# Weight sums of the third and fourth pair in the first feed-forward block: begun by ScalarE and DMA at the fetch instead of VectorE later

## The chip, the cores and the metric

The kernel runs on one core of a Trainium2 chip. A core has five engines that run their own queues in order: TensorE (PE, with its weight loads PEld), VectorE (DVE), ScalarE (ACT), GpSimd (POOL) and SyncE (SP). SP and POOL are used here to issue DMA transfers; a transfer that POOL issues can add what it reads to what already lies at its destination (an accumulating transfer). The metric is the device time of one execution in microseconds (us). One execution was also profiled, and its trace is what is read below.

## The reference

A bidirectional encoder trunk of two layers over 512 tokens and 16 learned meta tokens, width 1024, all in float32. Each layer is a feed-forward block, a mixer (gated linear attention beside softmax attention) and a second feed-forward block. What matters here is the feed-forward block, of which four run in one execution:

```python
def swiglu(x, w_gate, w_up, w_down):
    return (jax.nn.silu(x @ w_gate) * (x @ w_up)) @ w_down
...
    for l in range(DEPTH):
        h = h + 0.5 * swiglu(rmsnorm(h, norm_gains[l, 0]),
                             ffn_w_gate[l, 0], ffn_w_up[l, 0], ffn_w_down[l, 0])
        h = h + mixer(rmsnorm(h, norm_gains[l, 1]), w_in[l], gla_w2[l], gla_b2[l], gla_gn[l],
                      q_norm[l], k_norm[l], w_pa[l], w_pb[l], b_merge[l], w_out[l], cos, sin)
        h = h + 0.5 * swiglu(rmsnorm(h, norm_gains[l, 2]),
                             ffn_w_gate[l, 1], ffn_w_up[l, 1], ffn_w_down[l, 1])
    return rmsnorm(h, final_norm)[:, N_META:]
```

The inner width is 2816, which is 22 blocks of 128 columns.

## The kernel before

**Seven products instead of eight.** The 22 blocks of the inner width are taken as 11 pairs, numbered 0 to 10 (`NPAIR`); so the first four pairs are 0, 1, 2 and 3. For each pair the gate and up weights are cut into four tiles of 128 x 1024 that the host has laid out in DRAM: "11", "12", "21" and "22". Instead of eight products of these with the four parts of the input, seven products of sums are made, named "1" to "7". Product 1 takes tile 11, product 2 tile 12, product 4 tile 22. The other four take weight sums that the kernel makes on the chip:

- first sum, for product 5: s1 = 21 + 22
- third sum, for product 7: s3 = 21 - 11
- second sum, for product 6: s2 = 22 + s3
- fourth sum, for product 3: s4 = s2 - 12

The down projections of the first two groups of four pairs are done alike, as four-tile sets numbered 11 to 14.

**From float32 to the matrix unit.** Each of the seven operands becomes two tiles before TensorE reads it: ScalarE rounds it to a high part (`whi`, line 287) and VectorE subtracts that from the operand for a low part (`wlo`, line 288). One product is 24 matmuls (4 parts of the input, 2 halves, and hi x hi, hi x lo, lo x hi), with the two hi matmuls ahead of the first that reads `wlo`.

**Order.** `ffn_steps` writes the order of the products by hand. In the first block (layer 0, first feed-forward: `(0, 0)`) it begins, as (pair, product): (0,1) (0,2) (1,1) (1,2) (0,4) (1,4) (0,6) (0,5) (0,7) (0,3) (1,6) (1,5) (2,1) (1,7) (2,2) (1,3) (2,6) (2,5) (3,1) (2,7) (3,2) (2,4) (2,3) (3,6) (3,5) (3,7) and so on. The class `Weights` runs ahead of it: `use` makes the hi and lo parts 3 operands ahead of the product in hand (`make`) and fetches 9 ahead (`fetch`). A compile-time scheduler then sets the order on each engine's queue: by the order in the program, but passing over what it takes to be not ready yet by its own model of times. What it sets is fixed; on the chip each queue runs in that order and waits where something is late.

**Buffers.** Three raw tiles (`wraw`), three "long" tiles (`wsa`: s3 and s4 of the pairs) and three "short" tiles (`wsb`: s1 and s2). A new tile takes the place of one that is done with. In the first block the tile of s3 of pair 2 follows that of s4 of pair 0, which is free when product (0,3) has its `wlo`; that of s3 of pair 3 follows s3 of pair 1, free at the `wlo` of (1,7).

**How the sums are made.** There are two ways:

- Chained, for pairs 0 and 1 of every block: ScalarE writes s3 = -11 (`negative`, line 203); POOL issues a transfer that adds tile 21 from DRAM (line 208); tile 22 is loaded by SP as s2, and a second POOL transfer adds s3 to it. ScalarE also begins s4 as -12, and a third POOL transfer adds s2.
- By VectorE, for pairs 2 to 10: SP loads tile 21 as s3 (line 218) and tile 22 as s2 (line 219); when product 2's parts have been made VectorE subtracts tile 11 from s3 (line 253), which keeps tile 11 in its raw buffer until then; ahead of product 6's parts VectorE adds s3 to s2 (line 297), and behind them makes s4 (line 256).

In both, s1 is tile 21 loaded by SP with a POOL transfer that adds tile 22 (`first_sum`). In the pairs 0 and 1 of the first block the sums are begun when product 1's and 2's parts are made; in all others, `begin_sums` runs at the fetch of tile 11.

Of the kernel before, what the change touches and what calls it, by code (L numbers as in the profile page):

```python
# [148 lines left out]
NPAIR = FF // P // 2  # L149
# [21 lines left out]
class Weights:  # L171
# [34 lines left out]
    def add(self, t, src):  # L206

        self.nc.gpsimd.dma_start(t, src, accum_op=ALU.add)  # L208

    def begin_sums(self, f, i, w=None):  # L210

        got = self.summed
        s3 = None
        if i < 2:
            s3 = self.negative(f, i, "s3", w)
            self.add(s3, self.dram(f, i, "21"))
        elif i < NPAIR:
            s3 = self.block(f, i, "21", self.long, "wsa")
        s2 = self.block(f, i, "22", self.short, "wsb")
        if i < 2:  # L220
            self.add(s2, s3)
        got[f, i, "7"], got[f, i, "6"] = s3, s2
        if (f, i) not in OPENING:
            self.first_sum(f, i)
# [6 lines left out]
    def sums(self, f, i, product, w):  # L231


        got, V = self.summed, self.nc.vector
        if (f, i) in OPENING and product in "12":
            (self.begin_sums if product == "1" else self.first_sum)(f, i, *[w] * (product == "1"))
        if i < 2:
            if product == "2":
                s4 = self.negative(f, i, "s4", w)
                self.add(s4, got[f, i, "6"])  # L240
                got[f, i, "3"] = s4
        elif product == "1":
            if i < NPAIR:
                self.kept1 = w
            else:
                got[f, i, "7"] = self.negative(f, i, "s3", w)
                self.add(got[f, i, "7"], self.dram(f, i, "21"))
            if not i < NPAIR:
                self.add(got[f, i, "6"], got[f, i, "7"])
        elif product == "2":  # L250
            self.kept = w
            if i < NPAIR:
                V.tensor_tensor(got[f, i, "7"], got[f, i, "7"], self.kept1, ALU.subtract)
        elif product == "6":
            s4 = self.long.tile([P, SLAB], F32, tag="wsa", name=f"s4_{f[0]}{f[1]}_{i}")
            V.tensor_tensor(s4, w, self.kept, ALU.subtract)
            got[f, i, "3"] = s4
# [15 lines left out]
    def make(self, upto):  # L273
        nc = self.nc
        while self.made < min(upto, len(self.loads)):
            self.fetch(self.made + 1)
            s = self.made
            load = self.loads[s]
            w = self.raws.pop(s, None)
            if w is None:  # L280
                w = self.summed.pop(load)
            hi = self.hi_pool.tile([P, SLAB], F32R, tag="whi", name=f"whi{s}")
            lo = self.lo_pool.tile([P, SLAB], F32R, tag="wlo", name=f"wlo{s}")
            for a in np.split(np.arange(SLAB), 2 if s == 0 else 1):
                cs = slice(a[0], a[-1] + 1)
                with self.tc.issue_after(self.behind) if self.behind else nullcontext():
                    nc.scalar.copy(hi[:, cs], w[:, cs])  # L287
                nc.vector.tensor_tensor(lo[:, cs], w[:, cs], hi[:, cs].bitcast(F32), ALU.subtract)  # L288
            self.got[s] = (hi, lo)
            self.got.pop(s - 12, None)  # L290
            self.made += 1
            if not isinstance(load, int) and load[2] in "126":
                self.sums(*load, w)
            after = self.loads[s + 1] if s + 1 < len(self.loads) else 0
            if not isinstance(after, int) and after[2] == "6" and 2 <= after[1] < NPAIR:
                s2, s3 = [self.summed[after[:2] + (c,)] for c in "67"]
                nc.vector.tensor_tensor(s2, s2, s3, ALU.add)

# [30 lines left out]
def build(tc, ctx, xt, wts, win, par, w2, const, umask, out):  # L329
# [243 lines left out]
    def ffn(l, f, norm, done, following):  # L573

        x, rs, up, n = norm.x, None, None, live[0]
        w = n // 2
        pools = open_pools("left", psum=("s2",), c=4, s2=2)
        made, hid, sums, raw, sets = {}, {}, {}, {}, {}
        risen = iter(range(KC))

# [637 lines left out]
    def finish_chunk(c):  # L1218
        fin.square(c)
        gain(c, slice(0, SEQ))  # L1220

    def ending(sums, operand, rs):

        table("abs_reciprocal_sqrt_and_small")
# [146 lines left out]
```

## Time and profile before

| | |
|---|---|
| time, median of 3 runs | 2212.42 us (2210.72 to 2214.04) |
| the profiled execution's own time | 2211.05 us |
| its span, first to last instruction | 2209.2 us |
| DVE busy | 1785.4 us (81%) |
| ACT busy | 1214.1 us (55%) |
| POOL busy | 101.8 us (5%) |
| the first 40 us: DMA busy share of 16 engines | 0.92 and 1.05 in its two halves |

The profile gives for each instruction its start and duration in us, its engine, its line in the kernel, the operation, and the tiles as out<-in with their buffer numbers left out; so `wlo<-w,whi` is the low part of some operand `w`, and several kinds of tile share the name `w`. Behind a row, in brackets, stands how long the engine had been idle just before, and what ended that idle time. `SPq` and `ACTq` rows are DMA issues by an engine's sequencer. In the table by windows the columns are the stretch, its length, then the busy time and number of instructions of PE, PEld, DVE, ACT and POOL, the granted TensorE clock (1.00 is full speed), the mean busy share of the 16 DMA engines and GB/s.

### The profile page before, as it was taken

Reading aid. Unit: us, or ns where it says so; the run is one execution under the profiler, and the core shown is the slowest. Engines: PE = TensorE matmul, PEld = TensorE weight load, DVE = VectorE, ACT = ScalarE, POOL = GpSimd, SP = SyncE. Lnnn points to the kernel's source line nnn. Section 1 sums busy time; section 2 is a strip of 40 time slices with the busy share of each in tenths; the row PEclk is TensorE's granted clock in tenths of the full one; section 3 lists DMA queues with packets and bytes.
Section 4 is the critical chain, followed back from the end, with each engine's and each line's share of the span. In section 5 each row is a group of like instructions: output and inputs, shape, how many; then the busy total and the mean of one; then the engine's idle time right before and its main releaser. Section 6 shows DMA issues by size and latency. Waiting matters only on the chain.

```text
span 2209.2 us, 40079 instructions
## 1 busy us (share of the span) xinstructions
PE 2162.4 (98%) x16506; PEld 2070.2 (94%) x16506; DVE 1785.4 (81%) x2703; ACT 1214.1 (55%) x1779; POOL 101.8 (5%) x120
## 2 busy tenths in 40 slices
PE   7999999999999999999999999999999999999998
PEld 6999999989999999999999999999788888999997
DVE  7897978486886689889789979775879767997987
ACT  7544545344785555454575445453457836554543
POOL 1000000000000001000010000000000001000100
PEclk9999999999999999999999999999999999999999
DMA  9775753212113468666567757432121145776752
GB/s 268 189 204 160 191 152 106 82 49 68 49 39 122 114 167 205 190 182 187 162 163 186 207 164 191 143 110 77 49 84 51 42 133 152 198 202 181 189 165 67
DMA packets 87463, 311.41 MB, mean 141 GB/s; under 512 B 9712, under 2 KB 12144, under 8 KB 87280
## 3 DMA queue, kind: packets, MB, share of 16 engines
q1 hardware_dynamic: 68624, 245.53, 32.9%
q0 software_dynamic: 16704, 60.82, 15.8%
q8 instruction: 130, 2.13, 0.4%
q10 hardware_dynamic: 1952, 2.50, 0.4%
q14 instruction: 53, 0.43, 0.1%
HBM read 289.94 MB, written 2.10 MB: 132 GB/s over the span
## 4 chain that ended last, share of the span: by engine, by line
PE 81%; DVE 11%; ACT 4%; issue 2%; DMA 2%; SPq 0%; DVEq 0%; ACTq 0%
PE ss L598 37%; PE mm L465 13%; PE ss L712 11%; PE ss L465 10%; PE sm L465 2%; DVE wlo L288 2%; DMA w<-win 2%; PE sm L1074 1%; PE ss L1049 1%; DVE g L678 1%; ACT whi L287 1%; PE sm L1090 1%; DVE h L720 1%; PE ss L471 1%; PE sm L1091 1%
## 5 line engine op out<-in xcount | busy, mean ns | idle before, releaser
L598 PE MATMUL ss<-xc,whi 128*128 128x264 f32 (+1 forms) x4928 | 907.2, 285 | 15.5 <-ACT whi L287 7.4
L598 PEld LDWEIGHTS ss<-xc,whi 128*128 128x128 f32 x4928 | 767.2, 189 | 20.4 <-ACT c L602 8.4
L598 PE MATMUL ss<-xc,wlo 128*128 128x264 f32 (+1 forms) x2464 | 702.5, 285 | 8.8 <-DVE wlo L288 8.8
L598 PEld LDWEIGHTS ss<-xc,wlo 128*128 128x128 f32 x2464 | 466.5, 189 | 11.1 <-DVE wlo L288 10.9
L288 DVE TENSOR_TENSOR wlo<-w,whi 128x1024 fp32r<-128x1024 f32 (+1 forms) x337 | 408.1, 1217 | 63.4 <-ACT whi L287 63.2
L287 ACT CAST whi<-w 128x1024 fp32r<-128x1024 f32 (+1 forms) x337 | 350.0, 1050 | 163.3 <-PE ss L598 80.5
L465 PE MATMUL mm<-x,whi 128*128 128x264 f32 (+1 forms) x1712 | 384.6, 315 | 0.0
L465 PEld LDWEIGHTS mm<-x,whi 128*128 128x128 f32 x1712 | 278.3, 188 | 16.5 <-issue 1.0
L465 PE MATMUL mm<-x,wlo 128*128 128x264 f32 (+1 forms) x856 | 266.0, 315 | 0.0
L712 PE MATMUL ss<-g,whi 128*128 128x264 f32 (+1 forms) x1280 | 237.4, 284 | 0.0
L287 ACT CAST whi<-raw 128x1024 fp32r<-128x1024 f32 x126 | 132.3, 1050 | 163.4 <-PE mm L465 102.3
L602 ACT COPY c<-ss 128x528 f32<-128x528 f32 (+1 forms) x132 | 78.5, 594 | 258.6 <-PE ss L598 258.6
L288 DVE TENSOR_TENSOR wlo<-raw,whi 128x1024 fp32r<-128x1024 f32 x126 | 153.9, 1222 | 59.0 <-ACT whi L287 58.1
L712 PEld LDWEIGHTS ss<-g,whi 128*128 128x128 f32 x1280 | 198.4, 188 | 0.1
L712 PE MATMUL ss<-g,wlo 128*128 128x264 f32 (+1 forms) x640 | 181.3, 283 | 0.0
L465 PEld LDWEIGHTS mm<-x,wlo 128*128 128x128 f32 x856 | 159.6, 188 | 8.5 <-issue 0.7
L465 PE MATMUL ss<-g,whi 128*128 128x264 f32 (+2 forms) x900 | 166.3, 299 | 0.0
L465 PEld LDWEIGHTS ss<-g,whi 128*128 128x128 f32 x900 | 131.7, 188 | 5.3
L208 POOL DMA_DIRECT2D w<-win x60 | 52.7, 878 | 1574.7 <-DVE wlo L288 582.5
L712 PEld LDWEIGHTS ss<-g,wlo 128*128 128x128 f32 x640 | 120.5, 188 | 0.0
L444 ACT ACTIVATE c<-c 128x528 f32<-128x528 f32 (+1 forms) x88 | 56.6, 643 | 98.5 <-DVE c L642 98.4
L465 PE MATMUL ss<-g,wlo 128*128 128x264 f32 (+2 forms) x450 | 106.2, 300 | 0.0
(267 smaller groups left out, 3370.2 us busy)
## 6 DMA issues: line engine op xcount, KB each, us to landing
w<-win SPq DMA_DIRECT2D x335, 512.0 KB, 4.5
raw<-wts SPq DMA_DIRECT2D x126, 512.0 KB, 3.3
w<-win POOLq DMA_DIRECT2D x60, 512.0 KB, 7.4
s<-win POOLq DMA_DIRECT2D x24, 512.0 KB, 7.2
w<-s POOLq DMA_DIRECT2D x24, 512.0 KB, 5.6
s<-w POOLq DMA_DIRECT2D x8, 512.0 KB, 9.6
h<-xt SPq DMA_DIRECT2D x3, 528.0 KB, 6.8
out<-h ACTq DMA_DIRECT2D x4, 256.0 KB, 2.4
```

Of the source, the lines that this page charges most:

```text
L208: self.nc.gpsimd.dma_start(t, src, accum_op=ALU.add)
L287: nc.scalar.copy(hi[:, cs], w[:, cs])
L288: nc.vector.tensor_tensor(lo[:, cs], w[:, cs], hi[:, cs].bitcast(F32), ALU.subtract)
L444: prev_act[0] = S.activation(*args, **kw).ins
L465: TE.matmul(acc.half[i][:width], lhs, rhs[:, acc.spans[i]], start=first, stop=last)
L471: TE.matmul(a, weights, x[:, hs], start=True, stop=True)
L598: TE.matmul(acc[:, j], a[:, j, k], b[:, at], start=bool(begin and k == 0 and i == 0), stop=k == len(x) - 1 and i == 2, skip_group_check=no ...
L602: W.behind = S.copy(part(st, q), acc).ins
L678: V.tensor_tensor(r[into][:, ks], r[a][:, ks], r[b][:, ks], ALU.subtract)
L712: TE.matmul(acc[:, j], a[:, j, k], xs[b][:, k], start=bool(begin and k == 0 and i == 0), stop=k == 3 and i == 2, skip_group_check=not begin)
L720: V.tensor_tensor(to, to, acc, ALU.add)
L1049: TE.matmul(s[:n, i, :HF], lhs, kh[:, hs], start=True, stop=False)
```

## The change

The pairs 2 and 3 of the first block, and no others, are moved from the second way to the chained one for s3 and s2. `begin_sums` runs for them at the fetch of tile 11, so it now issues there: on ScalarE the negation of tile 11 into s3, on POOL the addition of tile 21 from DRAM into s3, on SP the load of tile 22 into s2, and on POOL the addition of s3 into s2. SP's load of tile 21 into s3 goes away, and so do VectorE's subtraction at line 253 and its addition at line 297. s1 and s4 of these pairs are made as before.

```diff
+    def chained(self, f, i):
+        return i < 2 or f == (0, 0) and i < 4
+
     def begin_sums(self, f, i, w=None):
 
         got = self.summed
         s3 = None
-        if i < 2:
+        if self.chained(f, i):
             s3 = self.negative(f, i, "s3", w)
             self.add(s3, self.dram(f, i, "21"))
         elif i < NPAIR:
             s3 = self.block(f, i, "21", self.long, "wsa")
         s2 = self.block(f, i, "22", self.short, "wsb")
-        if i < 2:
+        if self.chained(f, i):
             self.add(s2, s3)
         got[f, i, "7"], got[f, i, "6"] = s3, s2
...
-        elif product == "1":
+        elif product == "1" and not self.chained(f, i):
             if i < NPAIR:
                 self.kept1 = w
             else:
                 got[f, i, "7"] = self.negative(f, i, "s3", w)
                 self.add(got[f, i, "7"], self.dram(f, i, "21"))
-            if not i < NPAIR:
                 self.add(got[f, i, "6"], got[f, i, "7"])
         elif product == "2":
             self.kept = w
-            if i < NPAIR:
+            if i < NPAIR and not self.chained(f, i):
                 V.tensor_tensor(got[f, i, "7"], got[f, i, "7"], self.kept1, ALU.subtract)
...
-            if not isinstance(after, int) and after[2] == "6" and 2 <= after[1] < NPAIR:
+            if not isinstance(after, int) and after[2] == "6" and after[1] < NPAIR and not self.chained(*after[:2]):
                 s2, s3 = [self.summed[after[:2] + (c,)] for c in "67"]
                 nc.vector.tensor_tensor(s2, s2, s3, ALU.add)
```

## The prediction

> **What bounds the kernel now.** First the page, for the engine that sets the span.
>
> ```profile
> span 2209.2 us, 40079 instructions
> ...
> PE 2162.4 (98%) x16506; PEld 2070.2 (94%) x16506; DVE 1785.4 (81%) x2703; ACT 1214.1 (55%) x1779; POOL 101.8 (5%) x120
> ```
>
> TensorE is busy for 98% of the span, so the change can win only where TensorE stands still or runs slowly. I then read PE's timeline through the first block for idle time. Between 30 and 140 us three rows show more than 1 us of it.
>
> ```profile
> 40.65 1.13 PE L471 MATMUL ss<-t,const 128*128 128x264 f32 x4 [1.55 <-ACT whi L287]
> ...
> 53.58 0.59 PE L598 MATMUL ss<-xc,wlo 128*128 128x264 f32 x1 [3.15 <-DVE wlo L288]
> ...
> 69.34 0.39 PE L598 MATMUL ss<-xc,wlo 128*128 128x264 f32 x1 [2.36 <-DVE wlo L288]
> ```
>
> At 53.58 and 69.34 a product has its high part and waits for the low part from VectorE: 3.15 + 2.36 = 5.51 us. VectorE's timeline says why.
>
> ```profile
> 40.47 1.22 DVE L288 TENSOR_TENSOR wlo<-s,whi 128x1024 fp32r<-128x1024 f32 x1
> ...
> 45.28 1.22 DVE L288 TENSOR_TENSOR wlo<-w,whi 128x1024 fp32r<-128x1024 f32 x1
> ...
> 50.54 1.23 DVE L253 TENSOR_TENSOR w<-w,w 128x1024 f32<-128x1024 f32 x1 [3.42 <-DMA w<-win]
> 51.69 0.70 DVE L617 TENSOR_TENSOR c<-c 128x528 f32<-128x528 f32 x1
> 52.30 1.22 DVE L288 TENSOR_TENSOR wlo<-w,whi 128x1024 fp32r<-128x1024 f32 x1
> ...
> 55.80 1.22 DVE L288 TENSOR_TENSOR wlo<-s,whi 128x1024 fp32r<-128x1024 f32 x1
> 56.94 1.22 DVE L297 TENSOR_TENSOR w<-w,w 128x1024 f32<-128x1024 f32 x1
> ...
> 66.24 1.23 DVE L253 TENSOR_TENSOR w<-w,w 128x1024 f32<-128x1024 f32 x1 [4.92 <-DMA w<-win]
> ...
> 72.71 1.22 DVE L288 TENSOR_TENSOR wlo<-w,whi 128x1024 fp32r<-128x1024 f32 x1
> ```
>
> VectorE's queue stood 3.42 and 4.92 us at line 253, of pair 2 and of pair 3, with the low part that PE wanted queued behind it. What it waited for is the load of tile 21. The chain of waits has that load of pair 2 as one piece, issued the moment the 40.47 row frees its buffer (40.47 + 1.22 = 41.69):
>
> ```profile
> 41.72 8.73 DMA w<-win
> ```
>
> The stalls cost more than their length. The table by windows:
>
> ```profile
> 49.99:53.40 3.41, 0.44 (x4) 0.23 (x2) 2.86 (x3) 3.29 (x4) 0.00 (x0) 1.00 0.10 19
> 53.40:56.82 3.42, 3.24 (x14) 3.25 (x15) 3.42 (x5) 0.65 (x1) 0.07 (x1) 0.50 0.86 290
> ...
> 67.06:70.47 3.41, 1.13 (x9) 1.13 (x10) 3.41 (x6) 2.21 (x3) 0.00 (x0) 1.00 0.00 0
> 70.47:73.88 3.41, 3.41 (x17) 3.30 (x16) 3.41 (x5) 0.42 (x1) 0.00 (x0) 0.50 0.15 36
> ...
> 80.00:100.00 20.00, 20.00 (x166) 20.00 (x166) 18.64 (x27) 11.25 (x14) 1.76 (x3) 1.00 0.71 176
> ```
>
> Behind each stall the granted clock is 0.50 for one stretch of 3.41 us, with 14 and 17 matmuls where full speed (20.00 / 166 = 0.12 us each) gives 28. Half of the 3.24 busy us and of 3.41 us is 1.62 + 1.71 = 3.33 us. The place is worth 5.51 + 3.33 = 8.84 us.
>
> **The change part by part.**
>
> *Removed from VectorE:* two of line 253 at 1.23 us and two of line 297 at 1.22 us, and with the first two the waits. Without the one at 50.54, what is next for PE is the low part that ran at 52.30. Its high part is the first of two in this ScalarE row:
>
> ```profile
> 37.04 1.05 ACT L203 ACTIVATE s<-w 128x1024 f32<-128x1024 f32 x1
> ...
> 41.82 0.70 ACT L477 ACTIVATE rs<-ss,eps 128x528 f32<-128x528 f32 x1 [1.50 <-PE ss L471]
> ...
> 43.78 1.04 ACT L287 CAST whi<-w 128x1024 fp32r<-128x1024 f32 x1
> ...
> 48.56 2.00 ACT L287 CAST whi<-w 128x1024 fp32r<-128x1024 f32 x2 [0.66 <-DMA w<-win]
> ...
> 61.29 1.04 ACT L287 CAST whi<-w 128x1024 fp32r<-128x1024 f32 x1
> ...
> 90.18 1.05 ACT L287 CAST whi<-w 128x1024 fp32r<-128x1024 f32 x1
> ```
>
> It ends about 49.6, the low part then at 49.6 + 1.22 = 50.8. PE idled from 53.58 - 3.15 = 50.43, so about 0.4 us of the first stall stays; with line 617 (0.70) ahead, 1.1. If (0,3), whose operands are ready, runs first, nothing stays. I take 0.6. At the second place the high part ends at 61.29 + 1.04 = 62.33, and PE first asked at 69.34 - 2.36 = 66.98; nothing stays.
>
> *Added on ScalarE:* two negations at 1.05 us (37.04). The one of pair 2 needs tile 11, long landed, and the buffer freed at 41.69. ScalarE is idle for 1.50 us up to 41.82, so it fits there or, at the latest that I think likely, behind the 43.78 row: it ends between 42.75 and 44.82 + 1.05 = 45.9. Queued behind it, if it goes first, are the reciprocal root (line 477) and the cast at 43.78, both 42.75 - 41.82 = 0.93 us later; the cast's low part then ends at 45.28 + 1.22 + 0.93 = 47.4 instead of 46.5. PE did not wait for that low part, and the product before it covers an unknown share: the cost is between 0 and 0.9 us, and as no stall of PE shows near it I take 0.2.
>
> *Moved from SP to POOL:* per pair, one load leaves SP and two accumulating transfers join POOL's queue, the second waiting for the first to land. Prices from POOL's rows and landings (columns of the second fence: tile, queue, count, size, median us from issue to landing; the first row is the transfer at 36.48, the second those at 39.35 and 56.76, the third that at 43.35):
>
> ```profile
> 26.65 1.25 POOL L208 DMA_DIRECT2D s<-win  x1
> 36.48 0.87 POOL L208 DMA_DIRECT2D w<-s  x1 [8.57 <-DMA s<-win]
> 39.35 0.86 POOL L208 DMA_DIRECT2D w<-win  x1 [2.01 <-DVE t L503]
> 43.35 0.89 POOL L208 DMA_DIRECT2D s<-w  x1 [3.14 <-ACT rs L444]
> 56.76 0.88 POOL L208 DMA_DIRECT2D w<-win  x1 [12.52 <-DMA w<-win]
> ```
>
> ```profile
> w<-s POOLq DMA_DIRECT2D x1, 512.0 KB, 6.2
> w<-win POOLq DMA_DIRECT2D x2, 512.0 KB, 9.2
> s<-w POOLq DMA_DIRECT2D x1, 512.0 KB, 9.4
> ```
>
> Pair 1 ran this very chain: issued at 26.65 behind another accumulation, the sum landing at 36.48 + 6.2 = 42.7, 16.0 us in all. Over the whole page the medians are less:
>
> ```profile
> s<-win POOLq DMA_DIRECT2D x24, 512.0 KB, 7.2
> w<-s POOLq DMA_DIRECT2D x24, 512.0 KB, 5.6
> ```
>
> That is 12.8 us. For pair 2 I take 16.0, the nearest row, since two accumulations (39.35, 43.35) are under way then too. Issued between 42.8 and 45.9, s2 lands between 58.8 and 61.9 (by 12.8 from 55.6). Who wants it:
>
> ```profile
> 73.98 0.19 PEld L598 LDWEIGHTS ss<-xc,wlo 128*128 128x128 f32 x1 [0.21 <-DVE wlo L288]
> ...
> 79.70 0.41 PE L598 MATMUL ss<-xc,whi 128*128 128x264 f32 x2
> ```
>
> PE asked for the low part of (2,6) at 73.98 - 0.21 = 73.8; with 8.84 us won it asks at 64.9. Its casts take 1.05 + 1.22, so s2 must land by 62.7: covered by 0.8 to 3.9 us.
>
> Behind it on POOL is the addition into s1 of pair 2, for product (2,5). In the profile it landed at 56.76 + 9.2 = 66.0; now one more accumulation may stand ahead. Two in a row land (43.35 + 9.4) - (39.35 + 9.2) = 4.2 us apart, so it lands between 66.0 and 70.2. (2,5) starts at 79.70, then at 70.9; its high part takes 1.05, so 69.8 is in time: 0 to 0.4 us late, and up to 1.4 if the casts queue. I take 0.3.
>
> Pair 3 has room: its buffer is freed by the low part at 55.80 (57.0, then about 52), 16.0 us and two accumulations of 4.2 ahead bring s2 to 77, and its cast at 90.18 moves to 81.3. The load of tile 21 that leaves SP wins nothing more: SP's next issue waits for other buffers.
>
> *DMA work.* q1 and q0 in the page (packets, MB, share of the 16 engines):
>
> ```profile
> q1 hardware_dynamic: 68624, 245.53, 32.9%
> q0 software_dynamic: 16704, 60.82, 15.8%
> ```
>
> At 0.524 MB a transfer, a load takes 0.329 x 2209.2 / 469 = 1.55 us of all engines and an accumulation 0.158 x 2209.2 / 116 = 3.0. Each pair adds 6.0 - 1.55 = 4.5 us. The engines have this free: 90% of 49.99 to 53.40 and all of 67.06 to 70.47. If it were not free at the right time, it would delay s1 and s2 by up to 4.5; that is the second rival.
>
> *Sum.* 8.84 - 0.6 - 0.2 - 0.3 = 7.7, and 0.2 for the two more DMA transfers that share engines with the loads (between 0 and 4.5, nearer 0 since the free time lies at 50 and 67): 7.5 us. 2211.05 - 7.5 = 2203.55 for an execution like the profiled one, which lay 1.37 under the median; at the median 2212.42 - 7.5 = 2204.9. Bounds of the unknown prices: 8.84 with no residue (2203.6), 8.84 - 1.1 - 0.9 - 1.4 - 4.5 = 0.9 with all of them (2211.5).
>
> *The clock.* The windows show half clock behind stretches in which PE was busy 0.44 and 1.13 of 3.41 us. The Trainium skill, "TensorE: Matmul & The Clock Gate", Part 1, What's actually happening, has the clock halved after at least one idle window of about 3.4 us, the windows running freely. By that rule stalls of 3.15 and 2.36 us would not halve it, and the change would win 5.51 - 1.3 = 4.2 us. The trace disagrees: partly idle windows were enough.
>
> **The rivals.**
>
> 1. *The clock does not follow the stalls in most executions:* where a window begins relative to the stall decides it, and one trace shows one position. Then 5.51 - 1.3 = 4.2 is won: 2208.2. For it: the stall of 1.55 us at 40.65 is followed by no such stretch. Against: both stalls here were followed by it. 0.10.
> 2. *The sum arrives late:* DMA work of 4.5 us delays s2 or s1 of pair 2, so (2,6) or (2,5) stalls up to 4.5 us with perhaps half a clock window more: 7.5 - 3.5 = 4.0, 2208.4. For it: cover of 0.8 us at the near end. Against: that end needs the late negation and 16.0 together. 0.17.
> 3. *Slower: the negation comes late in ScalarE's queue.* The order is fixed at compile time by a model. From an end of 62.7 - 16.0 = 46.7 on, each us late costs PE one, plus 1.71 of half clock; the 8.2 left after the first residue is used up at an end of 53.2. Behind the cast at 61.29 (some 5 us earlier then, ending 57.5) it would end at 58.6: 11.9 + 1.7 against 8.2, 5.4 us slower, 2217.8. For it: no row shows the order that the model will set. Against: in the program it stands far ahead of that cast, and its operands are among the first ready. 0.12.
> 4. *The wait moves only:* VectorE's order changes so that another late operand heads its queue; what is won is given back, 2212. Nothing in the rows names such an operand. 0.08.
>
> **How the numbers follow.** The forecast (6 to 9 us) has 0.53. Range: 2202.5 (all won, 1 us of scatter as in the runs shown) to 2212.0, which leaves out the third rival and a little of the fourth. What a measurement can tell is 0.2%, 4.4 us: faster takes the forecast and half of the first two, 0.53 + 0.14 = 0.67; slower 0.11; same 0.22.
>
> **What would show it.** VectorE's rows before the low parts at 50 and 61 us without a wait; PE without the two idle times, and no half clock after 20 us; accumulations issued at 43 to 46 and landing 16 us on; the cast of (2,6) not waiting for a transfer. It is wrong if PE stalls on `whi` or `wlo` of (2,6) or (2,5), or if the negation of pair 2 ends after 47.

## The result and the profile after

| | before | after |
|---|---|---|
| median, 6 runs each | 2212.57 us (2208.98 to 2215.25) | 2203.36 us (2201.71 to 2204.51) |
| ratio, 95% interval | | 0.9958 (0.9946 to 0.997) |
| the profiled execution's own time | 2211.05 us | 2201.71 us |
| its span | 2209.2 us | 2199.8 us |

The change won 9.2 us between the medians, 6.6 to 11.9 by the interval. The forecast was 2204.9 us. Line numbers after are two higher than before: line 287 is 289, 288 is 290, 253 is 255, 598 is 600.

The head of the page after:

```profile
span 2199.8 us, 40087 instructions
...
PE 2158.0 (98%) x16506; PEld 2066.8 (94%) x16506; DVE 1781.3 (81%) x2699; ACT 1214.5 (55%) x1781; POOL 105.2 (5%) x124
```

The span is 9.4 us shorter: PE is busy 4.4 us less (2162.4 to 2158.0), and stands still 5.0 us less. PE's waits between 30 and 140 us, summed by what they waited for (us in total, times, longest), first before, then after:

```profile
PE ss L598 <- DVE wlo L288: 5.5, 2, 3.1
PE ss L471 <- ACT whi L287: 1.6, 1, 1.6
PE ss L598 <- ACT c L602: 0.5, 1, 0.5
```

```profile
PE ss L473 <- ACT whi L289: 2.0, 1, 2.0
PE ss L600 <- ACT c L604: 0.5, 1, 0.5
```

The two waits for a low part, 5.5 us, are gone; the wait at 40 us is 0.4 longer. Together 5.1, the 5.0 of the page. The table by windows after, over the stretch in which before had its two stalls and two half-speed stretches:

```profile
50.00:53.40 3.40, 3.40 (x29) 3.39 (x29) 3.40 (x5) 2.89 (x5) 0.83 (x1) 1.00 0.93 277
...
70.40:73.80 3.40, 3.40 (x30) 3.40 (x29) 2.71 (x4) 2.45 (x4) 1.10 (x2) 1.00 1.00 245
```

PE is never idle there and the clock is 1.00 with some 29 matmuls in 3.4 us. That accounts for 3.33 of the 4.4 us of busy time; the other 1.1 us was not followed further.

VectorE, ScalarE and POOL after, the rows that answer to those of the prediction:

```profile
49.26 1.22 DVE L290 TENSOR_TENSOR wlo<-w,whi 128x1024 fp32r<-128x1024 f32 x1
50.39 0.70 DVE L620 TENSOR_TENSOR c<-c,ss 128x528 f32<-128x528 f32 x1
51.01 1.22 DVE L290 TENSOR_TENSOR wlo<-w,whi 128x1024 fp32r<-128x1024 f32 x1
...
65.31 1.22 DVE L290 TENSOR_TENSOR wlo<-w,whi 128x1024 fp32r<-128x1024 f32 x1
```

```profile
44.03 1.04 ACT L203 ACTIVATE s<-w 128x1024 f32<-128x1024 f32 x1
44.97 1.03 ACT L289 CAST whi<-w 128x1024 fp32r<-128x1024 f32 x1
...
62.80 1.06 ACT L289 CAST whi<-w 128x1024 fp32r<-128x1024 f32 x1
```

```profile
45.47 0.88 POOL L208 DMA_DIRECT2D s<-win  x1 [1.20 <-ACT s L203]
52.57 0.87 POOL L208 DMA_DIRECT2D w<-s  x1 [6.22 <-DMA s<-win]
```

Up to 66 us no row of VectorE waits for a transfer now. The negation of pair 2 runs at 44.03 and ends at 45.07, between the reciprocal root's rows and the cast. Its accumulations start at 45.47 and 52.57; the second took 10.2 us to land (the table of DMA issues: `w<-s`, x1, 10.2), so s2 was there at 62.77, 17.3 us after the first issue. The cast of product (2,6) begins at 62.80, and PE does not wait for it.

### The profile page after: what moved, and what is told of

Read it like the earlier page. It is cut to its first block, busy times and chain, and to the rows that moved or that the text cites. A ratio compares the mean times of both kernels' runs of the same rounds, so it can differ in the third digit from the quotient of the medians.

```text
span 2199.8 us, 40087 instructions
## 1 busy us (share of the span) xinstructions
PE 2158.0 (98%) x16506; PEld 2066.8 (94%) x16506; DVE 1781.3 (81%) x2699; ACT 1214.5 (55%) x1781; POOL 105.2 (5%) x124
## 4 chain that ended last, share of the span: by engine, by line
PE 80%; DVE 12%; ACT 4%; issue 2%; DMA 2%; SPq 0%; DVEq 0%; ACTq 0%
PE ss L600 37%; PE mm L467 13%; PE ss L714 11%; PE ss L467 10%; PE sm L467 2%; DVE wlo L290 2%; DMA w<-win 2%; PE sm L1076 1%; DVE g L680 1%; ACT whi L289 1%; PE ss L1051 1%; PE ss L473 1%; ACT t L446 1%; DVE h L722 1%; DVE c L676 1%
```

## The experiments

The kernel before ran beside the others on the same chip: 2210.88 us (26 runs) for experiments 1 to 4, 2210.84 (25) for 5, 7 and 9, 2211.66 (12) for 6 and 8. Gains are counted against these.

**1. Only pair 2, and 2. only pair 3.**

```diff
-        return i < 2 or f == (0, 0) and i < 4
+        return i < 2 or f == (0, 0) and i == 2
```

The second kernel has `i == 3`.

> Only pair 2 has the second and third sum by negation and DMA additions; pair 3 is as before. Theory (each pair's gain is the wait at the head of VectorE's queue plus the half clock behind it, one stall for each pair): the stall of 3.15 us goes with its 1.6 to 1.7 us of half clock, 4.8 us won against before; the stall of pair 3 (2.36 us before VectorE's low part, VectorE waiting for the load of tile 21 of pair 3) stays with its 1.7 us, somewhere near 64 to 66 us; time about 1.1598 us short of nothing else: 2212.5 - 4.8 = 2207.7 us. Rival (the second stall is only the first one's after-effect, the load of pair 3 being late because pair 2 was): nearly all of the 9.2 us is won, 2203 to 2204. Rival (only the two together give the gain): within 1.5 us of before.

> Only pair 3 has the second and third sum by negation and DMA additions; pair 2 is as before. Theory: the stall of 3.15 us at 53.6 us stays with its half clock, the one at 69.3 us goes: 2.36 + 1.7 = 4.1 us won, 2208.4 us. Together with the kernel that has pair 2 alone the gains add up to that of the changed kernel within 1 us. Rival (the second stall follows from the first): 1.5 us or less is won, 2211 or above.

Measured: pair 2 alone 2210.31 us (11 runs), ratio 0.9999 (0.999 to 1.0008), nothing won. Pair 3 alone 2206.35 us (9 runs), ratio 0.9979 (0.9969 to 0.9989), 4.5 us won. By the medians the sizes do not add up: 0.6 + 4.5 against 7.6 to 9.2 for both. The intervals are too wide to show that by themselves, so the traces decide. Pair 2 alone, PE, VectorE and the windows (this execution took 2213.41 us, the slowest of the 11, and has one half-speed stretch more, behind its stall at 40.94):

```profile
70.99 0.59 PE L600 MATMUL ss<-xc,wlo 128*128 128x264 f32 x1 [6.99 <-DVE wlo L290]
```

```profile
67.89 1.23 DVE L255 TENSOR_TENSOR w<-w,w 128x1024 f32<-128x1024 f32 x1 [8.65 <-DMA w<-win]
...
69.72 1.22 DVE L290 TENSOR_TENSOR wlo<-w,whi 128x1024 fp32r<-128x1024 f32 x1
```

```profile
69.08:72.49 3.41, 1.50 (x7) 1.50 (x8) 3.41 (x6) 0.00 (x0) 0.00 (x0) 0.50 0.00 0
72.49:75.91 3.42, 3.42 (x17) 3.42 (x17) 3.42 (x5) 0.00 (x0) 0.00 (x0) 0.50 0.00 0
```

The first stall went, and the second grew from 2.36 to 6.99 us. VectorE waited 8.65 us at the subtraction of pair 3 for tile 21, whose load SP issued at 55.48. The table of DMA issues has it with 12.4 us to its landing, 9.2 before; the two accumulations of pair 2, issued at 53.18 and 54.68, were under way beside it:

```profile
w<-win SPq DMA_DIRECT2D x1, 512.0 KB, 12.4
```

PE ran out of work there at 70.99 - 6.99 = 64.00 us, 2.98 sooner than before (66.98), and the load landed at 67.86, 1.65 later than before (57.05 + 9.16 = 66.21). These two make up the 4.63 us by which the stall grew. Two half-speed windows followed. Both the theory (a fixed second stall) and its first rival (it goes by itself) were wrong: the first stall had been part of the second one's cover. The second rival had the time right, but not its reason, since pair 3 alone does win. Pair 3 alone keeps the first stall:

```profile
48.98 1.23 DVE L255 TENSOR_TENSOR w<-w,w 128x1024 f32<-128x1024 f32 x1 [2.01 <-DMA w<-win]
```

```profile
52.02 0.39 PE L600 MATMUL ss<-xc,wlo 128*128 128x264 f32 x1 [1.72 <-DVE wlo L290]
```

Up to here this kernel does what the one before does, yet VectorE waited 2.01 us in place of 3.42 and PE 1.72 in place of 3.15, as the load took 7.3 us (41.58 to 48.89) and not 8.73. The stall's length is a matter of the execution. No half-speed stretch follows it, against the theory, and this execution (2203.84 us) lies 2.5 us below its kernel's median; that the gain of 4.5 us met the forecast 4.1 is no proof of the theory's sum.

**3. The waiting subtraction moved, no chain.** The kernel before, with VectorE's subtraction of the pairs 2 and 3 issued behind the low part of that pair's product 1 (`issue_after` holds an instruction behind another one on the queues; `low1` is that low part, noted where it is made, which is left out here).

```diff
+                with self.tc.issue_after(self.low1) if f == (0, 0) and i < 4 else nullcontext():
-                V.tensor_tensor(got[f, i, "7"], got[f, i, "7"], self.kept1, ALU.subtract)
+                    V.tensor_tensor(got[f, i, "7"], got[f, i, "7"], self.kept1, ALU.subtract)
...
```

> The kernel before, with one difference: in the first block's pairs 2 and 3 VectorE's subtraction that waits for the load of tile 21 is issued behind the low part of that pair's product 1, no longer ahead of it. No DMA addition, no negation on ScalarE; SP issues the same loads. Theory (what cost the time was the place of the waiting subtraction at the head of VectorE's queue, and the chain by DMA is only one way to take it from there): both idle times of PE (3.15 and 2.36 us) and both stretches of half clock go, 2203 to 2205 us, as the changed kernel within 1.5 us; VectorE may still wait at that line, but with no low part behind it that PE wants. Rival (the gain needs the load of tile 21 and the two subtractions of each pair gone, because the sums come too late this way): a stall before product (2,6) or (2,5) comes back, 3 us or less are won, 2209.5 or above.

Measured: 2207.41 us (11 runs), ratio 0.9987 (0.9979 to 0.9996), 3.5 us won. In the trace both stalls and both half-speed stretches are gone, without a transfer added: PE is at 98.20 us where the changed kernel is at 98.39 (rows under 6). The subtraction of pair 2 runs at 53.70 behind three low parts and waits for nothing, as does that of pair 3 at 71.67; PE's list of waits from 36 to 130 us names no low part:

```profile
52.56 1.22 DVE L289 TENSOR_TENSOR wlo<-s,whi 128x1024 fp32r<-128x1024 f32 x1
53.70 1.22 DVE L254 TENSOR_TENSOR w<-w,w 128x1024 f32<-128x1024 f32 x1
```

So the place at the head of VectorE's queue was the cause of the stalls. The edit moves that subtraction alone, but the scheduler then set other rows in another order too (the cast of (2,2), at 61.29 before, runs at 54.06). And some 4 us were lost again behind 98 us; experiment 6 takes that up.

**4. Only s3 by the chain.** The changed kernel, with s2 again added by VectorE: two accumulations fewer.

```diff
-        if self.chained(f, i):
+        if i < 2:
             self.add(s2, s3)
...
```

> The changed kernel, but in pairs 2 and 3 of the first block only the third sum is made by negation and a DMA addition; the second sum is again VectorE's addition of the two, behind the low part of the product that its line names. Two accumulating transfers fewer. Theory (the wait for the load of tile 21 was all; the DMA addition of the second sum is not needed): 2203 to 2204.5 us, the same as the changed kernel within 1 us; that addition finds the third sum landed at about 52 us, and waits for it 1 us or less. Rival (the head of VectorE's queue now waits for the accumulation instead of the load): a wait of 2 to 4 us at that addition, PE idle behind it, 2206 to 2209 us.

Measured: 2203.27 us (6 runs), ratio 0.9967 (0.9955 to 0.9978), the same as the changed kernel.

```profile
53.70 1.22 DVE L290 TENSOR_TENSOR wlo<-s,whi 128x1024 fp32r<-128x1024 f32 x1
54.84 1.22 DVE L299 TENSOR_TENSOR w<-w,s 128x1024 f32<-128x1024 f32 x1
```

VectorE's addition finds s3 landed and does not wait; s2 is ready at 56.06, 6.7 us before the changed kernel's. The DMA addition of s2 wins nothing.

**5. The negation late, the prediction's third rival.** The changed kernel, with the negation of pair 2 and its additions issued behind the cast of product (2,1) (`late1`, shown without the lines that leave the negation out at the fetch) or (2,2) (`late2`).

```diff
...
+            if load == ((0, 0), 2, "1"):
+                s2 = self.summed[(0, 0), 2, "6"]
+                with self.tc.issue_after(high):
+                    s3 = self.negative((0, 0), 2, "s3", self.tile11)
+                self.add(s3, self.dram((0, 0), 2, "21"))
+                self.add(s2, s3)
```

> The changed kernel, with the negation of pair 2 held back on ScalarE until behind the cast of product (2,1), some 6 us later, its two accumulations with it. By the third rival of the prediction each us beyond an end at 46.7 us costs PE one, plus 1.71 us of half clock. Theory (that rule with the chain of 17.3 us from the changed kernel's trace): the negation ends at about 51, the sum lands at about 68.5, its cast ends at 69.6, and PE, which took its first matmul of (2,6) at 65.0, stands 4 to 5 us there: 2203.4 + 4.5 + 1.7 = 2209.6 us. Rival (the cover is longer than the rule says, since product (1,3) can fill the wait, or the chain is shorter with less beside it): under 2 us lost, 2205.5 or less.

> The changed kernel, with the negation of pair 2 held back until behind the cast of product (2,2), the slow case that the prediction's third rival names. Theory: the negation ends at about 59.5, the sum lands 17 us later at about 77, the high part at 78; PE has the products (2,2) and (1,3) ahead of it and runs out of work at about 69, so it stands 8 to 9 us, with 1.7 to 3.4 us of half clock behind: 2203.4 + 10 to 12.5 = 2213 to 2216 us, slower than before. Rival (the rule overstates: the chain takes about 13 us, the median over the page): a stall of 5 us, 2209 to 2211 us, not slower than before.

Measured: 2211.98 us (10 runs), ratio 1.0004 (0.9995 to 1.0013), and 2212.75 us (10 runs), ratio 1.0005 (0.9996 to 1.0014): all of the gain lost in both, and nothing beyond it that the intervals show. The first, on ScalarE, POOL and PE:

```profile
49.84 1.05 ACT L203 ACTIVATE s<-w 128x1024 f32<-128x1024 f32 x1
```

```profile
54.70 0.88 POOL L208 DMA_DIRECT2D w<-win  x1 [10.88 <-DVE h L770]
55.24 1.23 POOL L208 DMA_DIRECT2D s<-win  x1
66.71 0.87 POOL L208 DMA_DIRECT2D w<-s  x1 [10.24 <-DMA s<-win]
```

```profile
72.41 1.67 PE L609 MATMUL ss<-xc,whi 128*128 128x264 f32 x4 [7.30 <-ACT whi L291]
```

The negation ends at 50.89, 5.8 us later than in the changed kernel, but POOL issues the accumulation only at 55.24: its queue stood first at the addition into s1 (54.70). From there the chain takes 16.05 us (s2 lands at 71.29), the 16.0 that pair 1 had shown. s2 is 8.5 us later than the 62.77 of the changed kernel, and PE's stall 7.30 us: it had 1.2 us to spare. The theory missed POOL's queue and was 2.4 us short. In the second the negation ends at 58.49, the chain takes 13.7 us (58.89 to 72.58), and PE has the product (1,3), 2.9 us, ahead of its stall of 6.17 us. The edit did one thing more: the operands of pair 3 are fetched before that point, so its negation took the early place (44.36) and its accumulations (45.81 and 55.25) ran ahead of those of pair 2. Nothing else was moving beside the last accumulation, which took 4.4 us. PE's stall:

```profile
73.70 1.75 PE L609 MATMUL ss<-xc,whi 128*128 128x264 f32 x4 [6.17 <-ACT whi L291]
```

**6. POOL's order alone.** In experiment 3 ScalarE waited 3.06 us for a load, and POOL stood before it at an accumulation, behind which the addition into s1 of set 11 was queued:

```profile
103.10 1.06 ACT L203 ACTIVATE s<-w 128x1024 f32<-128x1024 f32 x1 [3.06 <-DMA w<-win]
```

```profile
93.32 0.88 POOL L208 DMA_DIRECT2D w<-s  x1 [7.26 <-issue]
93.95 1.16 POOL L208 DMA_DIRECT2D w<-win  x1
```

In the changed kernel these two stand the other way round, at 94.08 and 88.21. The edit gives the changed kernel experiment 3's order on POOL and leaves the order on ScalarE, VectorE and SP as it is (the line that leaves this addition out of its old place is not shown):

```diff
...
-                self.add(got[f, i, "6"], got[f, i, "7"])
+                added = self.add(got[f, i, "6"], got[f, i, "7"])
+                if f + (i,) == (0, 0, 11):
+                    with self.tc.issue_after(added):
+                        self.add(got[f, i, "5"], self.dram(f, i, "22"))
```

> The changed kernel with one difference: on POOL's queue the addition into s1 of set 11 stands behind the addition of s3 into s2 of that set, as in the kernel with the waiting subtraction moved; in the changed kernel the two stand the other way round. Theory (that kernel did remove both stalls and gave back about 2 us near 103 to 112 us because POOL's queue stood 7.5 us at that addition, which put the one behind it beside the loads): PE loses 1.5 to 2.5 us between 98 and 118 us, ScalarE waits 2 to 3 us there for a load; 2203.3 + 2 = 2205.3 us, and by chance at other places up to 1.7 us more. Rival (POOL's order is without weight, the loss came from VectorE's two waits at the load of tile 21 or from chance): 2202.5 to 2204.3 us, no idle time of PE over 0.6 us between 98 and 118 us.

Measured: 2205.03 us (6 runs), ratio 0.997 (0.9958 to 0.9982); the interval overlaps the changed kernel's, so the trace decides.

```profile
104.00 1.06 ACT L203 ACTIVATE s<-w 128x1024 f32<-128x1024 f32 x1 [2.49 <-DMA w<-win]
```

PE at the same two places of its queue, in the changed kernel, with POOL's order, and in experiment 3:

```profile
98.39 0.51 PE L600 MATMUL ss<-xc,whi 128*128 128x264 f32 x2 [0.50 <-ACT c L604]
223.06 0.51 PE L600 MATMUL ss<-xc,whi 128*128 128x264 f32 x2 [0.50 <-ACT c L604]
```

```profile
99.65 0.51 PE L604 MATMUL ss<-xc,whi 128*128 128x264 f32 x2 [0.50 <-ACT c L608]
225.85 0.51 PE L604 MATMUL ss<-xc,whi 128*128 128x264 f32 x2 [0.50 <-ACT c L608]
```

```profile
98.20 0.52 PE L601 MATMUL ss<-xc,whi 128*128 128x264 f32 x2 [0.50 <-ACT c L605]
224.94 0.51 PE L601 MATMUL ss<-xc,whi 128*128 128x264 f32 x2 [0.50 <-ACT c L605]
```

That is 124.67, 126.20 and 126.74 us: POOL's order costs 1.5 of the 2.1 us that experiment 3 lost there. The other 2 of the 4 us that it lacks by the medians are not settled: its one trace has a half-speed stretch at 562 us (1.7 us, below), and such stretches come and go between executions.

**7. Every block.** `return i < 4`: the pairs 2 and 3 chained in all four feed-forward blocks.

> Pairs 2 and 3 chained in all four feed-forward blocks, not only in the first. Theory (the gain comes only from where VectorE's waiting subtraction stood ahead of a low part that PE wanted; no row of PE after 100 us shows more than 1.1 us of idle time, so there is nothing to win): the same as the changed kernel within 1.5 us, 2202.5 to 2205 us. Rival A (the VectorE time and the load saved are worth something everywhere): 1 us or more won in each further block, 2200.5 or less. Rival B (accumulations stretch the loads beside them, as in the kernel with pair 2 alone, where the load of tile 21 of pair 3 took 12.4 us): the further blocks lose 1 us each or more, 2206.5 or above.

Measured: 2206.02 us (9 runs), ratio 0.9976 (0.9966 to 0.9986), 2.8 us worse than the changed kernel. The intervals overlap, but the fastest of its nine runs, 2205.37 us, is slower than ten of the changed kernel's eleven. Nothing is won in the other blocks, as the theory said, but something is lost, and not by rival B's way. ScalarE and PE in the second block:

```profile
793.13 1.06 ACT L203 ACTIVATE s<-w 128x1024 f32<-128x1024 f32 x1 [2.52 <-DVE wlo L290]
794.10 0.58 ACT L604 COPY c<-ss 128x528 f32<-128x528 f32 x1
```

```profile
794.73 0.52 PE L600 MATMUL ss<-xc,whi 128*128 128x264 f32 x2 [1.50 <-ACT c L604]
```

The negation stands on ScalarE ahead of the copy of a product out of PSUM (the memory that TensorE writes to), and waits there for its buffer; PE waits for the copy.

**8. These negations held back** behind that copy, by a few operands, in the three later blocks.

> Pairs 2 and 3 chained in all four blocks as before, but in the three later blocks each of their negations is issued on ScalarE a few operands later, behind the copy of a product out of PSUM that it had stood ahead of. Theory (the 2.8 us that the kernel with every block chained lost against the changed kernel came from these negations at the head of ScalarE's queue: PE waited there 1.50, 0.88 and 1.60 us for the copy at 794.7, 1165.9 and 1876.0 us, where the changed kernel has 0.69, 0 and 0.68): 2203 to 2204.5 us, and the three waits as in the changed kernel. Rival (the loss is the DMA work of six more chains, 4.5 us of all engines each): 2205.5 or above, the waits of PE on loads or on accumulations.

Measured: 2206.63 us (7 runs, 2203.32 to 2209.12), ratio 0.9974 (0.9963 to 0.9985). In the trace the wait at that place is the changed kernel's again (0.69 us at 794.89 in experiment 9's trace), and so are those at the other two places, 0 and 0.68 us where every block chained had 0.88 and 1.60:

```profile
794.91 0.51 PE L610 MATMUL ss<-xc,whi 128*128 128x264 f32 x2 [0.69 <-ACT c L614]
```

The median is not restored. So the queue place explains those three waits, but not the loss of the time; what keeps the median up was not found.

**9. The changed kernel again.**

> The changed kernel itself once more, beside the kernels of this call. Theory (the gain is real and the profiled execution was a usual one): 2202.5 to 2204.5 us, ratio 0.995 to 0.998. A second trace of it tells whether the place of the half clock is the same in each execution: if it follows the stall, the stall of 2.00 us at 40.9 us is followed by full clock again; if it depends on how a free-running grid of 3.41 us lies over the stall, the half clock may appear there (as it did in one of the traces at a stall of 1.81 us) or not.

Measured: 2203.23 us (5 runs), ratio 0.9964 (0.995 to 0.9978), 7.6 us won. At 40.46 us PE stalls 1.81 us, with full clock behind it, as in the first trace; a half-speed stretch stands at 561 us, where the first trace has none (last section).

## Why the prediction was right

The forecast of 7.5 us stands beside measured gains of 9.2 and 7.6 us, and inside both intervals. The mechanism held; that 7.5 meets 7.6 so closely is partly luck, as small losses were taken off that did not come, and the half clock stands in the sum in full. By its own steps:

- *What bounds the place.* VectorE's queue standing at line 253 with a wanted low part behind it: shown by experiment 3, in which the edit moved only that subtraction, without a transfer added, and both stalls went. 5.51 us of idle time was right; 5.1 net was measured.
- *The half clock, 3.33 us.* Right in size for the two traces compared. That it belongs to every execution is too simple: by the bound found below, stalls of 3.15 and 2.36 us are followed by half clock about nine and six times in ten, which makes some 2.6 us on average (an estimate from 1.7 us for each).
- *Residues of the first stall, 0.6, of the delayed cast, 0.2, of s1, 0.3.* All were 0: no row of PE shows an idle time there. The low part was there at 49.26 + 1.22 = 50.48 in the trace after, as its cast began at 48.04, not 48.56, without the wait for a load. s1 landed at 54.19 + 12.3 = 66.5, inside the forecast 66.0 to 70.2, and (2,5) was not asked for before 71.15.
- *DMA work, 0.2.* The free time of the DMA engines at 50 and 67 us, on which this rested, is not there in the trace after: they are 0.93 busy from 50.00 to 53.40 and 0.96 from 67.00 to 70.40. No wait of PE came of it.
- *The chain.* 16.0 us was forecast and 17.3 measured. The second accumulation ran beside other transfers (the table by windows has 0.93 to 1.05 of the 16 engines in the four stretches from 50.00 to 63.60); which of them made it longer was not tested. The negation ended at 45.07, inside the forecast 42.75 to 45.9. s2 came at 62.77 against a limit of 62.7 and stalled nothing: the limit was 1.3 us too early. It put both casts before the first ask. PE's first matmuls of (2,6) run at 65.03 and need the high part alone, for which 65.03 - 1.05 = 63.98 is in time; the low part is made at 65.31.
- *Rival 1 (the clock)* stands as half true: the grid's place decides, but the stalls of before were long enough to be hit more often than not. *Rival 2 (late sum)* did not come, by 1.2 us. *Rival 3 (late negation)* was forced in experiment 5: all of the gain is gone with an end at 50.89, where it put the break-even at 53.2, since POOL's queue added 4 us that the prediction did not count. Further on it overstated the loss: an end at 58.49 cost no more, with (1,3) in between, a chain of 13.7 us in place of 16.0, and pair 3's chain already done. *Rival 4 (a moved wait)* did not come in the changed kernel, but it did for pair 2 alone, where the operand that headed the queue was pair 3's own tile 21.

What the prediction lacked, without harm to the sum: the two stalls are not two terms. Each is what is left of a load's time after the work ahead of it, so the first one covered the second. The 8.84 was right because both went together.

## What to carry to other kernels

A subtraction that waits for a transfer at the head of an in-order queue costs what stands behind it. Ask first whether it can stand later in the queue: that alone took both stalls away here, though only 3.5 us were won, as the order behind it cost some again. A chain through ScalarE and POOL won more, and brings new queues in which the same can happen (POOL behind another accumulation, ScalarE ahead of a copy that PE wants). Take away one stall of two and see whether the other grows: stalls in a row on the same kind of load are not independent sums.

## What the runs showed of the hardware

*The half clock comes from a grid of windows that lies differently in each execution.* The clock's record begins at 18 to 23 us; from there all half-speed stretches of one trace lie whole multiples of 3.41 us apart (before: 70.47 - 53.40 = 17.07, five of them). Two kernels stalled 1.81 us at the same place of the program. The windows of each trace's own grid over that stall (for the second counted back 153 steps from its stretch at 560.98), first experiment 4, then the changed kernel again:

```profile
37.14:40.55 3.41, 1.60 (x13) 1.41 (x12) 3.10 (x5) 2.62 (x4) 0.86 (x1) 1.00 1.06 288
40.55:43.96 3.41, 3.41 (x13) 3.00 (x13) 0.84 (x1) 1.59 (x3) 0.82 (x1) 0.50 0.95 239
```

```profile
38.75:42.16 3.41, 1.70 (x11) 1.60 (x11) 2.55 (x3) 1.66 (x3) 0.86 (x1) 1.00 0.97 253
42.16:45.57 3.41, 3.41 (x31) 3.41 (x29) 1.78 (x3) 3.34 (x5) 1.42 (x2) 1.00 0.70 150
```

With 1.60 of 3.41 us busy the next window ran at half clock, with 1.70 at full, and in the trace of pair 3 alone with 1.62 (38.24 to 41.65) too: the bound lies near half. A stall of about 1.8 us thus costs 1.7 us more or nothing, about one time in two, and one of 3.15 about nine times in ten (an estimate: a stall counts when at least 1.8 us of it fall into one window, and the grid is taken to lie at random). The Trainium skill, "TensorE: Matmul & The Clock Gate", Part 1, What's actually happening, has windows of 3.413 us that run freely, and the clock halved after at least one idle window. These traces bear out the first and not the second: here windows that were nearly half busy sufficed. Nor is it busy time alone: in the same trace the half-speed stretch at 561 us follows a window in which PE was busy throughout, part of it with matmuls of 2 and 16 columns; 4 of the 12 traces have a stretch there (561 to 569 us). What sets it off is open.

```profile
557.57:560.98 3.41, 3.41 (x31) 3.39 (x30) 1.89 (x5) 2.01 (x6) 0.00 (x0) 1.00 0.00 0
560.98:564.39 3.41, 3.41 (x18) 3.34 (x17) 2.83 (x9) 2.05 (x5) 0.00 (x0) 0.50 0.00 0
```

*A transfer takes longer beside others.* The load of pair 3's tile 21 took 9.2 us beside one accumulation (the kernel before) and 12.4 us beside two (experiment 1); as other loads were under way both times and each is a single transfer, that the second accumulation was the cause is not shown. One accumulation of 512 KB took 4.4 us with nothing beside it (the last in `late2`), 12.3 as s1 of pair 2 in the changed kernel, and 13.0 as the same s1 in experiment 1.
